# A hybrid encoder trunk in one program: the convolution's layer norm in two stages, w_out's split spread over attention units, and three more taps off VectorE

## The chip, the cores and the metric

The kernel runs on one core of one Trainium2 chip, as one launch. The metric is the device time of the launch in microseconds, as the median of several executions. A profile of one execution gives the trace from which all durations come; its span runs from the first instruction to the last. In the profile PE is TensorE's matmuls, PEld its weight loads, DVE is VectorE, ACT is ScalarE, POOL is GpSimd and SP issues the DMAs.

## The reference, cut to what matters

One layer of an encoder, run for a prompt of 512 rows and a sample of 1024 rows with the same weights, model width 1024:

```python
h = rmsnorm(x, norm_attn_g)
z = h @ w_in                                   # q, k, v, ca, cb
a_out = window_attn(q, k, v, bias, band, sink) # 8 heads of 64, blocks of 128, each sees 3 blocks
c = ca * sigmoid(cb)
c = dwconv(c, conv_dw_w, conv_dw_b)            # 31 taps along the rows, 512 channels
c = silu(layernorm(c, conv_ln_g, conv_ln_b))   # over the 512 channels of a row
x = x + concat(a_out, c) @ w_out
h = rmsnorm(x, norm_ffn_g)
u = dwconv(h @ w_up, ffn_dw_w, ffn_dw_b)       # 3 taps, 2 x 2816 channels
x = x + (silu(u[:, :2816]) * u[:, 2816:]) @ w_down
y = rmsnorm(x, norm_final_g)
```

All of it is float32. The kernel makes each float32 product from three matmuls of rounded parts: a high part, and a low part that is the rest (`hi*hi + hi*lo + lo*hi`). So every operand of a product is split first: a cast on ACT gives the high part, a subtraction on POOL or DVE the low part.

## The kernel before, in words

The work is cut in blocks of 128 rows: blocks 0 to 3 are the prompt, 4 to 11 the sample. An attention unit u is one block (u // 2) and one of two key heads (u % 2), so units 0 to 7 are the prompt's and 8 to 23 the sample's.

**Stages.** First come the input projections of the prompt, then those of the sample with the prompt's attention, convolution norm and output projection between them. Then follows the prompt's FFN up-projection, 22 steps (`ffn_step`), with the sample's attention between its matmuls. Behind it come the sample's output projections (`out_half`), the convolution norms of its later blocks, and the FFN of the sample, whose order is written out by hand and which the change does not touch.

**Side work.** Work beside the main stream is written as generators that yield between pieces. `proj`, the loop over 24 matmuls of a projection, calls `tick()` three times, and its caller once more. A tick adds `rate` to a due count and advances the first generator of `side` for each whole one; and it adds a credit, of which each convolution item takes its cost of 0.66. `convs` holds the items of the prompt, `late` those of the sample, which are served when `convs` is empty. The program order that comes out is laid onto the engines' queues by a planner that works ahead of time with its own timeline; on the chip each engine's queue is in order.

**Convolution.** `conv_items(g, c, cp)` makes one column block of 128 channels and 512 rows: 31 taps less `NOFF[g]` are `scalar_tensor_tensor` on DVE into a PSUM bank (L339), the last `NOFF[g]` are a scaling on ACT (L328, L331) and an add on POOL (L332). The result goes to DRAM (`cvd`).

**Convolution norm.** `conv_norm(i)` loads one block of `cvd` (L669), transposes it (L675), takes statistics on DVE (L677, L678) and the inverse root on POOL (L173, L174), scales on DVE (L681), yields twice (`YN`), transposes back (L687), applies gain, bias and silu on ACT and DVE (L690 to L693) and splits (L694, L695) into `cats[i, 1]`. For the prompt it first drains `convs`. It is called whole: behind units 4 to 7 for blocks 0 to 3, for blocks 4 and 5 behind the sample's attention (`NE` = 2), and for block i + 2 beside the output projection of block i.

**Attention and w_out.** `attention(u0, u1, then)` runs `scores(u + 1)`, `values(u)`, then the generator `then[u]`. `w_out` has 16 tiles of 128 x 512; each is loaded (L736, L738) and split (`split_wo`, L740, on ACT and POOL through L189 and L190). For the sample, `sample()` does this in one loop after all attention units, five loads ahead of the splits (`WOA`). `w_up` is split by the same L189 and L190, one half of a column block after each half of an FFN step.

**Memory.** SBUF tiles come from counted slots; h is the class of 61 slots of 2 KB. PSUM is eight banks, of which projections take two, attention and norm three to five.

Of the kernel before, what the change touches and what calls it, by code (L numbers as in the profile page):

```python
# [36 lines left out]

RA, RB, RBO, RD, RN, RE = 1.2, 0.8, 2.5, 0.8, 0.95, 0.9  # L40


CA, CB = 0.9, 0.4
CL, CLO, CD = 0.6, 1.0, 0.6

NOFF = (4, 7)

SCB, SCD = "aapa", "aaap"


WOP, WOA, DW, DW2 = 1, 5, 2, 0
NE = 2
YN = 2
OB = "uc"
VG = 3
NW = 36
KEEP = 3
U0 = 2

# [83 lines left out]
def tile_hybrid_encoder(ctx: ExitStack, tc: tile.TileContext, xs, rel_bias, norm_attn_g, w_in,  # L143
# [9 lines left out]

    sb = Slots(big, dict(q=(15, 4096), c=(4, 4224), h=(61, 2048), d=(2, 2176), s=(32, 64)), "q", KEEP)
    banks = Slots(lambda tag: ps[two_of[tag]], dict(a=(3, 2048), u=(2, 2048), b=(2, 2048), c=(1, 2048)))
    use = dict(step="aub", turn="aub", conv="c", attn="au", norm="b", out="b", up="u", down="b")
# [4 lines left out]
    def bank(job):  # L161
        return banks.tile([NT], among=use[job])
# [51 lines left out]
    def rows_T(parts, out):  # L214
        r = sb.tile([P])
        n = 0
        for src, k in parts:
            nc.sync.dma_start(r[n:n + k, :], src)
            n += k
        pt = bank("step")  # L220
        nc.tensor.transpose(pt[:, :n], r[:n, :], ident[:n, :n])
        nc.vector.tensor_copy(out, pt[:, :n])
# [3 lines left out]
    rows_T([(rw(norm_attn_g), 8)], vecs[:, 0:8])  # L226
    for _ in range(NW // 4):
        pt = bank("step")
        for i in range(4):
            nc.tensor.transpose(pt[:, i * P:(i + 1) * P], ident[:], ident[:])  # L230
        pt = None
# [33 lines left out]
    side, pace = deque(), dict(rate=0.0, due=0.0, conv=0.0, credit=0.0, late=0.0)  # L265

    def advance(queue):
        try:
            return next(queue[0])
        except StopIteration:  # L270
            queue.popleft()
            return 0.0
# [15 lines left out]
    def drain(queue):  # L288
        while queue:
            advance(queue)  # L290
# [24 lines left out]
    def conv_items(g, c, cp):  # L315
        T = GR[g]["T"]
        w = lambda t: cvw[:, t * 4 + c:t * 4 + c + 1]
        cost = 0.13 + NT / 960.0
        noff = NOFF[g]
        off = list(range(CK - noff, CK))  # L320
        for n in range(T // NT):
            src = lambda t: cp[:, t + n * NT:t + (n + 1) * NT]
            pacc = sb.tile([NT])

            def offload(k):
                t = off[k]
                if k == 0:
                    nc.scalar.activation(pacc[:], src(t), AF.Identity, scale=w(t))  # L328
                else:
                    pr = sb.tile([NT])  # L330
                    nc.scalar.activation(pr[:], src(t), AF.Identity, scale=w(t))  # L331
                    nc.gpsimd.tensor_tensor(pacc[:], pacc[:], pr[:], op=ALU.add)  # L332

            acc = bank("conv")
            nc.vector.tensor_scalar(acc[:], src(0), w(0), cvb[:, c:c + 1], op0=ALU.mult, op1=ALU.add)
            yield cost
            k = 0
            for t in range(1, CK - noff):
                nc.vector.scalar_tensor_tensor(acc[:], src(t), w(t), acc[:], op0=ALU.mult, op1=ALU.add)  # L339
                if t % 2 == 1 and k < noff:  # L340
                    offload(k)
                    k += 1
                yield cost
            while k < noff:
                offload(k)
                k += 1
            nc.vector.tensor_tensor(pacc[:], acc[:], pacc[:], op=ALU.add)
            del acc
            nc.sync.dma_start(cvd[g][:, c, n * NT:(n + 1) * NT], pacc[:])
            yield cost  # L350

    tanh_t, cpads, kt, vt = {}, {}, {}, {}
# [150 lines left out]
    bias = []  # L503
# [12 lines left out]
    NB = len(blocks)  # L516
    qt, cats, units = {}, {}, {}
# [13 lines left out]
    score_rows = []  # L531

    def sink_columns():
        for h in range(0, NH, 2):
            t = sb.tile([2, NT])
            for n in range(2):
                nc.vector.tensor_copy(t[:, n, 0:1], nsink[:, h + n:h + n + 1])
            score_rows.append(t)
# [60 lines left out]
    def cat_of(i, part):  # L599
        if (i, part) not in cats:  # L600
            cats[i, part] = (sb.tile([4, P], F32R), sb.tile([4, P], F32R))
        return cats[i, part]
# [46 lines left out]
    def attention(u0, u1, then={}):  # L649
        yield from scores(u0)  # L650
        for u in range(u0, u1):
            if u + 1 < u1:
                yield from scores(u + 1)
            yield from values(u)
            if u in then:
                yield from then[u]

    def load_cat(i):
        cats[i, 0] = (sb.tile([4, P], F32R), sb.tile([4, P], F32R))
        for L in range(2):  # L660
            nc.sync.dma_start(cats[i, 0][L][:].bitcast(F32), catd[blocks[i][1], :, L, :].rearrange("p (j t) -> p j t", t=P))

    def conv_norm(i):
        G, b = blocks[i]
        if G["g"] == 0:
            drain(convs)
        cat = cat_of(i, 1)
        cv = sb.tile([4, P])
        nc.sync.dma_start(cv[:], cvd[G["g"]][:, :, b * P:(b + 1) * P])  # L669
        if G["g"] == 1 and (i, 0) not in cats:  # L670
            load_cat(i)
        yield 0.0
        pt = bank("norm")
        for c in range(4):
            nc.tensor.transpose(pt[:, c * P:(c + 1) * P], cv[:, c, :], ident[:])  # L675
        st, mv, rs = sm(6), sm(2), sm(1)
        nc.vector.bn_stats(st[:], pt[:])  # L677
        nc.vector.bn_aggr(mv[:], st[:])  # L678
        rstd_of(mv[:, 1:2], 1.0, rs[:])
        xh = sb.tile([CCH])  # L680
        nc.vector.tensor_scalar(xh[:], pt[:], mv[:, 0:1], rs[:], op0=ALU.subtract, op1=ALU.mult)  # L681
        del pt
        for _ in range(YN):
            yield 0.0
        p2 = bank("norm")
        for c in range(4):
            nc.tensor.transpose(p2[:, c * P:(c + 1) * P], xh[:, c * P:(c + 1) * P], ident[:])  # L687
        y, t = sb.tile([4, P]), sb.tile([4, P])
        for c in range(4):
            nc.scalar.activation(y[:, c, :], p2[:, c * P:(c + 1) * P], AF.Identity,  # L690
                                 scale=lng[:, c:c + 1], bias=lnb[:, c:c + 1])
        nc.scalar.activation(t[:], y[:], AF.Tanh)
        nc.vector.scalar_tensor_tensor(t[:], t[:], 1.0, y[:], op0=ALU.add, op1=ALU.mult)  # L693
        nc.scalar.copy(cat[0][:], t[:])  # L694
        nc.vector.tensor_tensor(cat[1][:], t[:], cat[0][:].bitcast(F32), op=ALU.subtract)  # L695
        yield 0.0
# [70 lines left out]

    use.update(step="b", turn="a", attn="au", norm="au", out="u")

    def prompt():  # L770
        yield from attention(0, 8, {u: conv_norm(u - 4) for u in range(4, 8)})
        kt.clear(), vt.clear(), qt.clear(), bias.clear()
        pace.update(rate=RBO, late=CLO)
        for n in range(2):
            for kc in range(KC):
                if (kc, n) not in wor:
                    load_wo(kc, n)
            yield 0.0
            for kc in range(KC):
                split_wo(kc, n, kc % 2 < DW)  # L780
                if kc % 2 == 1:
                    yield 0.0
            for i in range(4):
                if n == 0 and i == 3:
                    for kc in range(WOP):
                        load_wo(kc, 1)
                yield from out_half(i, n)
            wo.clear()
        yield from make_h2(0, 0)
# [107 lines left out]
        want_up(0, half)  # L897
    want_up_raw(1, 0)
    load_bias()
    def sample():  # L900
        sink_columns()
        yield from attention(8, 24)
        kt.clear(), vt.clear(), qt.clear(), bias.clear(), score_rows.clear()
        use.update(norm="a")
        pace.update(rate=RN)
        for m in range(16 + WOA):
            if m in (10, 12):
                load_cat(m // 2 - 1)
            if m < 16:
                load_wo(m // 2, m % 2)  # L910
            if m >= WOA:
                split_wo((m - WOA) // 2, m % 2, m % 4 < DW2)
                yield 0.0
        drain(late)
        for m in range(NE):
            yield from conv_norm(4 + m)

    pace.update(rate=RD, late=CD)
    for k in range(NJ):
# [159 lines left out]
    pace.update(rate=2.2)  # L1079
    for i in range(4, NB - 2):  # L1080
        if i + NE < NB:
            side.appendleft(conv_norm(i + NE))
        if i == 8:
            pace.update(rate=RE)
            side.appendleft(turned(1, old_bank))
        for n in range(2):
            out_blocks(i, n)
# [155 lines left out]
    for j in range(2):  # L1243
        st[j] = dict(x=wide())
        prod(st[j]["x"][:, L], j, 1, True, True)
        a = sb.tile([NT])
# [322 lines left out]
    u, e, o11, o12 = (acc.pop(n) for n in ("u", "e", "o11", "o12"))  # L1569
# [73 lines left out]
```

## Time and profile before

| | us |
|---|---|
| median of 3 runs (lowest, highest) | 1564.2 (1560.03, 1566.33) |
| the profiled execution's own time | 1558.91 |
| its span | 1557.1 |
| TensorE busy | 1506.9 (97%) |
| VectorE busy | 1126.2 (72%) |
| ScalarE busy | 795.4 (51%) |
| GpSimd busy | 708.9 (46%) |

The granted clock of TensorE is 0.990 of full speed over the span. A row of a group has a line, an engine, an operation, output and inputs by name, and a count; then durations, or the idle time before them and what ended it. Where windows are shown, each gives its length, then for each engine the busy time and in brackets the instructions, then the granted clock, the share of the DMA engines' time and GB/s.

### The profile page before, as it was taken

How to read it: one execution, taken by the hardware profiler on the slowest of the kernel's cores; microseconds unless marked ns; L12 is line 12 of the kernel's file. 1: busy time of each engine (PE TensorE's matmuls, PEld its weight loads, DVE VectorE, ACT ScalarE, POOL GpSimd, SP SyncE). 2: the span in 40 equal slices, each digit the busy share in tenths (PEclk: the TensorE clock that was granted, in tenths of full speed). 3: DMA queues.
4: the chain of work that ended last, by engine and by line, in shares of the span. 5: the costliest groups of instructions: out<-in, count | busy, mean ns of one | idle time of the engine just before them, and what ended most of it. 6: DMA issues, size and time to landing. Idle time of an engine off the chain costs nothing. (4 is left out here: it accounts for less than half of the span.)

```text
span 1557.1 us, 20112 instructions
## 1 busy us (share of the span) xinstructions
PE 1506.9 (97%) x6843; PEld 1229.4 (79%) x6843; DVE 1126.2 (72%) x1604; ACT 795.4 (51%) x1404; POOL 708.9 (46%) x566
## 2 busy tenths in 40 slices
PE   8899998999999999899999999999999999999997
PEld 6787787787888888777777888888888788888885
DVE  7999767857788785344868777777776845568883
ACT  4634654335787786633454444455545543444254
POOL 7652344226666776947433455555554000003355
PEclk9999999999999999999999999999999999999999
DMA  7582334447343346779332233333331582356644
GB/s 230 156 212 81 107 100 124 129 142 217 112 132 129 118 129 181 242 238 298 114 93 76 92 104 104 105 104 102 102 115 64 200 284 82 105 165 230 221 135 162
DMA packets 228780, 227.17 MB, mean 146 GB/s; under 512 B 13268, under 2 KB 168348, under 8 KB 228549
## 3 DMA queue, kind: packets, MB, share of 16 engines
q1 hardware_dynamic: 228677, 225.88, 45.8%
q8 instruction: 54, 0.88, 0.2%
q14 instruction: 49, 0.40, 0.1%
HBM read 164.74 MB, written 62.14 MB: 146 GB/s over the span
## 5 line engine op out<-in xcount | busy, mean ns | idle before, releaser
L190 POOL TENSOR_TENSOR q<-q,q 128x1024 fp32r<-128x1024 f32 x72 | 173.4, 2415 | 93.4 <-ACT q L189 34.4
L940 POOL TENSOR_TENSOR q<-q,q 128x512 fp32r<-128x512 f32 x101 | 140.0, 1391 | 164.0 <-ACT q L1050 151.7
L940 DVE TENSOR_TENSOR h<-h,h 128x512 fp32r<-128x512 f32 (+2 forms) x202 | 153.9, 794 | 65.2 <-ACT h L944 25.3
L1398 PE MATMUL w<-h,h 128*128 128x512 f32 x462 | 181.4, 393 | 1.4 <-DVE q L1185 1.4
L1399 PE MATMUL w<-h,h 128*128 128x512 f32 x462 | 181.5, 393 | 0.0
L1400 PE MATMUL w<-h,h 128*128 128x512 f32 x462 | 181.1, 392 | 0.0
L1064 PE MATMUL w<-h,q 128*128 128x512 f32 x448 | 176.5, 394 | 1.0 <-ACT h L1147 0.6
L1066 PE MATMUL w<-h,q 128*128 128x512 f32 x448 | 175.5, 392 | 1.0 <-POOL q L940 1.0
L1065 PE MATMUL w<-h,q 128*128 128x512 f32 x426 | 166.4, 391 | 0.0
L296 PE MATMUL u<-h,q 128*128 128x512 f32 x400 | 161.0, 403 | 5.4 <-DVE h L837 4.1
L297 PE MATMUL u<-h,q 128*128 128x512 f32 x400 | 158.6, 397 | 0.0
L299 PE MATMUL u<-h,q 128*128 128x512 f32 x384 | 151.8, 395 | 2.7 <-POOL q L190 2.7
L937 POOL TENSOR_TENSOR q<-q,q 128x1024 f32<-128x1024 f32 x12 | 32.4, 2707 | 236.6 <-DVE q L937 220.0
L339 DVE SCALAR_TENSOR_TENSOR c<-c,cvw,c 128x512 f32<-128x512 f32 x184 | 138.0, 750 | 2.9
L944 ACT CAST h<-h 128x512 fp32r<-128x512 f32 x120 | 71.9, 619 | 93.2 <-DVE h L940 41.9
L296 PE MATMUL b<-h,q 128*128 128x512 f32 x256 | 102.7, 401 | 3.3 <-DVE d L369 2.2
L1398 PEld LDWEIGHTS w<-h,h 128*128 128x128 f32 x462 | 86.8, 188 | 21.6 <-ACT h L944 1.8
L1400 PEld LDWEIGHTS w<-h,h 128*128 128x128 f32 x462 | 86.7, 188 | 19.7
L1399 PEld LDWEIGHTS w<-h,h 128*128 128x128 f32 x462 | 86.8, 188 | 19.5
L837 DVE SCALAR_TENSOR_TENSOR h<-u,fw,h 128x511 f32<-128x511 f32 x88 | 65.5, 744 | 49.8 <-ACT h L841 49.0
L299 PE MATMUL b<-h,q 128*128 128x512 f32 x256 | 101.4, 396 | 0.0
L297 PE MATMUL b<-h,q 128*128 128x512 f32 x256 | 101.1, 395 | 0.0
(417 smaller groups left out, 3670.4 us busy)
## 6 DMA issues: line engine op xcount, KB each, us to landing
q<-in_w_up SPq DMA_DIRECT2D x88, 512.0 KB
ga<-q SPq DMA_DIRECT2D x64, 256.0 KB
h<-ga SPq DMA_DIRECT2D x57, 256.0 KB
q<-in_w_in SPq DMA_DIRECT2D x28, 512.0 KB
h<-in_w_down SPq DMA_DIRECT2D x52, 256.0 KB
q<-in_x_sample SPq DMA_DIRECT2D x15, 512.0 KB
h<-qsd SPq DMA_DIRECT2D x24, 256.0 KB
x1d<-q SPq DMA_DIRECT2D x11, 512.0 KB
```

The source lines that it names most:

```text
L190: (nc.vector if dve else nc.gpsimd).tensor_tensor(lo[:], raw[:], hi[:].bitcast(F32), op=ALU.subtract)
L296: nc.tensor.matmul(out, whi[:, kc, :], hi[:], start=(kc == 0), stop=False)
L297: nc.tensor.matmul(out, whi[:, kc, :], lo[:], start=False, stop=False)
L299: nc.tensor.matmul(out, wlo[:, kc, :], hi[:], start=False, stop=(kc == KC - 1))
L339: nc.vector.scalar_tensor_tensor(acc[:], src(t), w(t), acc[:], op0=ALU.mult, op1=ALU.add)
L940: (eng or nc.vector).tensor_tensor(out, a, b, op=ALU.subtract)
L1064: nc.tensor.matmul(out, whi[:, s], hi[:], start=(start and c == 0), stop=False, **go)
L1065: nc.tensor.matmul(out, whi[:, s], lo[:], start=False, stop=False, **go)
L1066: nc.tensor.matmul(out, wlo[:, s], hi[:], start=False, stop=(stop and c == 3), **go)
L1398: nc.tensor.matmul(out, sh[:, c], th[:], start=(p == 0), stop=False)
L1399: nc.tensor.matmul(out, sh[:, c], tl[:], start=False, stop=False)
L1400: nc.tensor.matmul(out, sl[:, c], th[:], start=False, stop=(p == NPAIR - 1))
```

## The change

`conv_norm` is cut in two. `conv_norm_1` runs up to the scaled rows, which it keeps in `normed`; `conv_norm_2` transposes them back and does the rest. For the prompt, the first stage of block i stands behind unit i + 3, the second behind unit i + 4, ahead of the next block's first. For the sample, the first stages of blocks 4 and 5 follow the splits, then second and first stages alternate, two blocks apart; beside the output projection of block i stand the second stage of i + 2 and the first of i + 4.

The loop over w_out's tiles becomes a generator, of which two pieces are taken behind each of units 19 to 23 and the rest after the attention.

`NOFF` goes from 4 to 7 for the prompt's four column blocks, and from 7 to 10 for the first two of the sample's (both halves of the rows). Convolution credits for the sample go from 0.6, 1.0 and 0.6 a tick to 0.45, 0.8 and 0.62; the side rates `RD` and `RN` from 0.8 and 0.95 to 0.84 and 0.9.

```diff
-RA, RB, RBO, RD, RN, RE = 1.2, 0.8, 2.5, 0.8, 0.95, 0.9
+RA, RB, RBO, RD, RN, RE = 1.2, 0.8, 2.5, 0.84, 0.9, 0.9
-CL, CLO, CD = 0.6, 1.0, 0.6
-NOFF = (4, 7)
+CL, CLO, CD = 0.45, 0.8, 0.62
+NOFF = ((7, 7, 7, 7), (10, 10, 7, 7))
-YN = 2
+WOU = 19
-        noff = NOFF[g]
+        noff = NOFF[g][c]
+    normed = {}
     def conv_norm(i):
+        yield from conv_norm_1(i)
+        yield from conv_norm_2(i)
+    def conv_norm_1(i):
...
         nc.vector.tensor_scalar(xh[:], pt[:], mv[:, 0:1], rs[:], op0=ALU.subtract, op1=ALU.mult)
-        del pt
-        for _ in range(YN):
-            yield 0.0
+        normed[i] = xh
+        yield 0.0
+    def conv_norm_2(i):
+        cat, xh = cat_of(i, 1), normed.pop(i)
         p2 = bank("norm")
...
     def prompt():
-        yield from attention(0, 8, {u: conv_norm(u - 4) for u in range(4, 8)})
+        yield from attention(0, 8, {u: both(*([conv_norm_2(u - 4)] if u > 3 else []), *([conv_norm_1(u - 3)] if u < 7 else []))
+                                    for u in range(3, 8)})
...
-    def sample():
-        sink_columns()
-        yield from attention(8, 24)
-        kt.clear(), vt.clear(), qt.clear(), bias.clear(), score_rows.clear()
-        use.update(norm="a")
-        pace.update(rate=RN)
+    def wo_pieces():
         for m in range(16 + WOA):
...
+    def some(gen, n):
+        for _ in range(n):
+            if next(gen, None) is None:
+                return
+            yield 0.0
+    def sample():
+        sink_columns()
+        wos = wo_pieces()
+        yield from attention(8, 24, {u: some(wos, 2) for u in range(WOU, 24)})
+        kt.clear(), vt.clear(), qt.clear(), bias.clear(), score_rows.clear()
+        use.update(norm="a")
+        pace.update(rate=RN)
+        yield from wos
         drain(late)
+        yield from conv_norm_1(4)
+        yield from conv_norm_1(5)
         for m in range(NE):
-            yield from conv_norm(4 + m)
+            yield from conv_norm_2(4 + m)
+            if NE + 4 + m < NB:
+                yield from conv_norm_1(4 + NE + m)
...
         if i + NE < NB:
-            side.appendleft(conv_norm(i + NE))
+            side.appendleft(both(conv_norm_2(i + NE), *([conv_norm_1(i + NE + 2)] if i + NE + 2 < NB else [])))
```

More of the change, by code (lines that the diff above doesn't have):

```diff
@@ L666, in conv_norm @@
             drain(convs)
-        cat = cat_of(i, 1)
         cv = sb.tile([4, P])
@@ L768, in tile_hybrid_encoder, with both @@
     use.update(step="b", turn="a", attn="au", norm="au", out="u")
+    def both(*gens):
+        for g in gens:
+            yield from g
     def prompt():
-        yield from attention(0, 8, {u: conv_norm(u - 4) for u in range(4, 8)})
+        yield from attention(0, 8, {u: both(*([conv_norm_2(u - 4)] if u > 3 else []), *([conv_norm_1(u - 3)] if u < 7 else []))
+                                    for u in range(3, 8)})
         kt.clear(), vt.clear(), qt.clear(), bias.clear()
```

## The prediction

> **What bounds the kernel now.** I read the page's busy times first, then the list of what TensorE waited for, then the windows around the waits, and last the timeline inside the two worst windows.
>
> ```profile
> PE 1506.9 (97%) x6843; PEld 1229.4 (79%) x6843; DVE 1126.2 (72%) x1604; ACT 795.4 (51%) x1404; POOL 708.9 (46%) x566
> ```
>
> TensorE is busy 1506.9 of 1557.1 us, so nothing that leaves its 6843 instructions alone can win more than the 50.2 us in which it stands, plus what it loses at a lowered clock. The change adds and removes no TensorE instruction. It can only fill holes or make new ones, and only up to the last convolution norm's activation:
>
> ```profile
> L690 ACT ACTIVATE h<-a,vecs x36: 441/457/488, 240.8 to 764.6; 128x128 f32<-128x128 f32 x36
> ```
>
> That is at 764.6 us. The list of TensorE's waits names the holes (wait, total, times, longest):
>
> ```profile
> PE u L296 <- DVE h L837: 4.1, 2, 3.5
> PE u L687 <- DVE q L681: 4.0, 1, 4.0
> PE u L687 <- DVE h L681: 2.9, 1, 2.9
> PE u L711 <- DVE s L678: 2.2, 1, 2.2
> PE b L296 <- DVE d L369: 2.2, 1, 2.2
> PE u L616 <- DVE s L567: 2.0, 2, 1.1
> PE a L560 <- DVE s L567: 1.7, 1, 1.7
> PE a L675 <- DMA h<-cvd: 1.4, 1, 1.4
> PE b L987 <- DVE q L958: 1.0, 1, 1.0
> ```
>
> L687 are the second transposes of the convolution norm, which wait for the normalised rows of L681. L711 is the output projection, which comes right behind a norm. L296 behind L837 is an up-projection waiting for its PSUM bank. The windows show what each place costs in all (length, then busy times of PE, PEld, DVE, ACT, POOL, the granted clock, DMA):
>
> ```profile
> 267.00:281.00 14.00, 7.03 (x27) 5.35 (x25) 6.60 (x12) 8.32 (x17) 7.67 (x9) 0.63 0.39 118
> 281.00:290.00 9.00, 9.00 (x40) 7.27 (x40) 6.48 (x11) 4.95 (x9) 0.75 (x2) 1.00 0.75 228
> 560.00:629.00 69.00, 69.00 (x341) 57.81 (x341) 46.06 (x94) 52.67 (x102) 49.34 (x30) 1.00 0.56 169
> 629.00:665.00 36.00, 31.91 (x136) 25.36 (x135) 11.89 (x18) 20.00 (x32) 35.84 (x26) 0.95 0.71 225
> 680.00:690.00 10.00, 7.81 (x34) 6.22 (x33) 6.00 (x9) 4.70 (x9) 6.06 (x9) 0.83 1.05 370
> 730.00:740.00 10.00, 8.55 (x43) 6.76 (x42) 4.43 (x6) 1.77 (x3) 5.09 (x7) 1.00 0.97 311
> 740.00:750.00 10.00, 8.32 (x41) 6.41 (x40) 6.33 (x9) 5.03 (x11) 5.66 (x9) 1.00 0.65 217
> ```
>
> **The prompt's norms (L663 to L695).** The timeline of 267 to 280 us, block 2's norm (start, duration, engine, line):
>
> ```profile
> 267.06 0.60 PE L675 MATMUL a<-ident,q 128*128 128x128 f32 x4
> 268.60 1.26 POOL L332 TENSOR_TENSOR q<-q,q 128x512 f32<-128x512 f32 x1 [3.29 <-ACT q L331]
> 270.22 0.57 POOL L174 TENSOR_TENSOR s<-s,nhalf 128x1 f32<-128x1 f32 x1
> 270.83 0.81 DVE L681 TENSOR_SCALAR q<-a,s,s 128x512 f32<-128x512 f32 x1 [2.21 <-POOL s L174]
> 271.69 1.12 PE L687 MATMUL u<-ident,q 128*128 128x128 f32 x4 [4.03 <-DVE q L681]
> 272.85 1.50 ACT L690 ACTIVATE h<-u,vecs 128x128 f32<-128x128 f32 x4 [2.23 <-PE u L687]
> 276.61 1.09 PE L687 MATMUL u<-ident,h 128*128 128x128 f32 x4 [2.94 <-DVE h L681]
> 279.70 0.60 ACT L373 ACTIVATE h<-b 128x512 fp32r<-128x512 f32 x1
> ```
>
> The two transposes stand next to each other on TensorE with a whole chain between them: statistics, the root on POOL behind a convolution add (L332), the scaling on DVE. Projections cannot fill the gap, because their bank is emptied by L373, which sits in ACT's queue behind L690, which waits for L687. That is a knot of in-order queues, and it is tied twice, for blocks 2 and 3.
>
> What does it cost? The 14.00 us hold 27 TensorE instructions. Sixteen are transposes, 0.60 us for four at full clock (row at 267.06). Eleven are matmuls, at 9.00/40 = 0.225 us each when nothing is missing (281 to 290). That is 2.4 + 2.5 = 4.9 us of work, so 9.1 us are lost, 6.97 of them standing and the rest at the clock of 0.63.
>
> The change puts an attention unit between the stages: L687 of block i comes directly behind values(i+4), with its rows ready since values(i+3). The second stage of one block then meets only the first stage of the next. Nothing is added but a held tile per block. Both waits on L681 should go. What stays is the ACT work ahead of L373 (L690 and three more for each block), so I leave 2.6 us of the 9.1 and book **-6.5** (bounds -9.1, where all goes, and 0, where the knot is tied at another place). Next in the queue is then the output projection, 5 ticks earlier in program order, because the two stages together yield 12 times where the old norm yielded 16 times.
>
> **w_out's splits (L740, cast L189 and subtract L190).** Sixteen splits come in one run behind the attention, and POOL is busy 35.84 of 36.00 us there. ACT suffers with it:
>
> ```profile
> 651.70 0.62 ACT L189 CAST h<-h 128x512 fp32r<-128x512 f32 x1 [1.32 <-DMA h<-in_w_out]
> 653.26 0.77 ACT L841 ACTIVATE h<-u,vecs,fw 128x512 f32<-128x512 f32 x1
> 655.75 0.76 PE L296 MATMUL u<-h,q 128*128 128x512 f32 x1 [3.45 <-DVE h L837]
> ```
>
> ACT stands 1.32 us for a w_out tile that has not landed, behind it wait L841 and L837, and TensorE waits for the bank they free. The window loses 4.09 us standing and 0.05 x 36 = 1.8 at the lowered clock, 5.9 in all. The change moves ten of the sixteen splits to units 19 to 23, with loads two or three units ahead: 5.9 x 10/16 = **-3.7** (bounds -5.9 and 0). The cover of the moved work is POOL's and ACT's idle time at 560 to 629 us: a split is one L190 on POOL, so ten are 13.0 us by the row below, against 69.00 - 49.34 = 19.7 us idle; 16.3 us of ACT are idle there, too. If that cover fails, see the second rival.
>
> **The norms of the sample.**
>
> ```profile
> 684.95 0.47 PE L711 MATMUL u<-h,h 128*128 128x512 f32 x1 [2.19 <-DVE s L678]
> 685.25 0.40 PE L712 MATMUL u<-h,h 128*128 128x512 f32 x1
> 687.84 0.63 PE L711 MATMUL u<-h,h 128*128 128x512 f32 x1
> ```
>
> In 680 to 690 us stand 12 transposes (1.8 us) and 22 matmuls (4.95), so 3.2 us are lost: 2.19 standing and 1.0 to the slow matmuls behind it (0.63 against 0.40). The norms of blocks 4 and 5 will be finished and those of 6 and 7 begun when the first output projection starts, and w_out is done 30 matmuls earlier. I book **-2.5** (bounds -3.2 and 0). In 730 to 750 us 3.1 us stand open, but the list's two waits there, L675 for the convolution's rows (1.4) and L987 for a DVE scaling (1.0), stay where they are: **-0.5** (bounds -3.1 and +1).
>
> The clock behind a hole is where trace and skill part. The Trainium skill (TensorE: Matmul & The Clock Gate, "HAM oscillation — how this bites in real kernels") says that gaps longer than about 3.4 us bring the slow clock; by that the 2.19 us gap would cost only itself, this term would be -1.5, and the sum 1.0 us less. Here the row at 687.84 shows slow matmuls behind it, so the measurement decides.
>
> **Taps.** Twelve taps of the prompt and twelve of the sample leave DVE and become a scaling on ACT and an add on POOL:
>
> ```profile
> L339 DVE SCALAR_TENSOR_TENSOR c<-c,cvw,c x184: 714/752/758, 184.2 to 575.8; 128x512 f32<-128x512 f32 x184
> L331 ACT ACTIVATE h<-c,cvw x38: 707/722/737, 230.4 to 581.2; 128x512 f32<-128x512 f32 x38
> L332 POOL TENSOR_TENSOR h<-h,h x47: 1278/1297/2162, 41.5 to 585.5; 128x512 f32<-128x512 f32 x47
> L190 POOL TENSOR_TENSOR h<-h,h x16: 1282/1302/1314, 629.2 to 664.9; 128x512 fp32r<-128x512 f32 x16
> ```
>
> Per twelve: DVE -9.0 us (0.752 each), ACT +8.7 (0.722), POOL +15.6 (1.297). For the sample they fall, by the order of ticks, beside the prompt's output projections and before the sample's attention; in 281 to 290 us POOL is busy 0.75 of 9.00 us there, ACT 4.95: 0. For the prompt they fall ahead of 190 us. There TensorE waits 5.9 us for DVE (2.2 + 2.0 + 1.7 in the list), which could shrink, but POOL's weight splits stand in the queue with the added adds: six adds of the first two channel blocks are 7.8 us. The convolution's credit per tick is as before, so DVE is as dense as before and only done sooner (forced out 8 ticks earlier, with 10 taps left, not 17). I take **0** (bounds -5.9 and +7.8; nearer the first row, as the taps run in a spare queue most of the time).
>
> ```profile
> 50.39 0.75 DVE L247 TENSOR_SCALAR q<-q,s 128x1024 f32<-128x1024 f32 x1 [0.44 <-POOL s L174]
> 60.48 2.40 DVE L247 TENSOR_SCALAR q<-q,s 128x1024 f32<-128x1024 f32 x1
> ```
>
> The same scaling took 0.75 and, beside a POOL split, 2.40 us, which speaks against more work on POOL; but the taps of L339 stay within 714 to 758 ns whatever POOL does, so only the few L247 can be hit. The Trainium skill (SBUF — State Buffer, "SBUF: two separate sides") has DVE and POOL lock a shared port for a whole instruction; were every DVE instruction hit, the 15.6 us would outweigh the 9.0 by 6.6 and the sum would be 6.6 us smaller. The rows of L339 say otherwise.
>
> **The rest.** New rates and credits add no instruction: 0. Any of these edits reorders the queues up to 765 us, and tiles are held longer (ten early pieces take some 25 of the 61 small tiles, of which 17 to 28 are free in units 19 to 23, so SP's w_out loads may wait for a slot with w_up loads behind them). I allow for two new waits like those of L616, 1.0 each: **+2.0** (bounds 0 and +6).
>
> **Sum.** -6.5 - 3.7 - 2.5 - 0.5 + 0 + 2.0 = -11.2 us. The profiled execution took 1558.9 us, 1.8 around its span of 1557.1; it would take 1547.7. The median of the runs shown is 1564.2, 5.3 above the profiled one, so I put the same difference on the median: **1553.0 us**.
>
> **Rivals.** *The knot stays.* The second stage meets another in-order wait, or the first stage's L675 takes the wait, and the prompt gains nothing: -4.7, 1559.5 us. For it: the queues' order is worked out ahead of time, and in front of L687 stands whatever its plan thinks ready. Against: L681 would be finished a whole unit before L687.
>
> *POOL becomes the bound in units 19 to 23: slower.* Two splits per unit put 2.60 us in POOL's queue, and if they stand ahead of a w_up split, TensorE waits for it.
>
> ```profile
> 603.34 2.41 POOL L190 TENSOR_TENSOR q<-q,q 128x1024 fp32r<-128x1024 f32 x1 [5.37 <-issue]
> 610.41 0.39 PE L296 MATMUL u<-h,q 128*128 128x512 f32 x1
> ```
>
> A w_up split that ends at 605.75 is used at 610.41: 4.66 us of lead. It decides from the point where the splits and whatever queues behind them eat that lead. Then each of five units costs 2.6 us standing and 1.0 of slow clock behind it, 18.0 in all, and the sample's gains fail too as POOL is late again at 629: 18.0 - 6.5 = +11.5, 1575.7 us. Against: POOL's 19.7 idle us there, and the lead.
>
> *Every hole closes:* 9.1 + 5.9 + 3.2 + 3.1 + 5.9 = 27.2 off, 1537.0 us.
>
> **How the numbers follow.** A measurement of this kernel can tell about 0.5%, 7.8 us, from no change. The forecast has 0.55 (0.02 of it above 1556.4), the knot 0.20, POOL 0.20, all holes 0.05. Faster: 0.55 - 0.02 + 0.05 = 0.58; same: 0.22; slower: 0.20. The forecast's own range is 1544 to 1562 (prompt gain 0 to 9.1, taps -5.9 to +4). To leave out no more than 2 in 10, I go from 1540, which drops most of the last case, to 1574, which drops half of POOL's: 0.15 left out.
>
> **What would show it.** Right: no wait of L687 for L681 in the prompt, the clock at 1.00 from 267 to 281 us, POOL clearly under 36 of 36 us around 629 to 665, no wait of L296 for L837 and none of L711 behind a norm, with DVE's busy time down by 18 and POOL's up by 31 us. Wrong: TensorE waiting for L190 at 560 to 629 us, new waits in front of L675, or a sum of TensorE's standing time ahead of 765 us no smaller than now.

## The result, and the profile after

The changed kernel takes **1577.3 us** (median, 1573.1 to 1578.7) against 1562.9 us of the kernel before (four runs of each): a ratio of **1.0086 [1.0061, 1.0111]**, slower. The profiled execution took 1576.8 us; its span is 1574.9, 17.8 longer than before.

The busy line of the page and the list of what TensorE waited for, of the kernel after:

```profile
PE 1518.0 (96%) x6843; PEld 1237.1 (79%) x6843; DVE 1115.5 (71%) x1580; ACT 811.4 (52%) x1428; POOL 739.6 (47%) x590
```

```profile
PE u L296 <- DVE h L851: 8.7, 3, 7.1
PE u L560 <- DMA h<-qsd: 3.9, 1, 3.9
PE u L560 <- DVE q L640: 3.9, 1, 3.9
PE u L720 <- ACT h L189: 3.3, 1, 3.3
```

Of the 17.8 us, TensorE's busy time holds 11.1 (1518.0 against 1506.9 for the same 6843 instructions, at a mean granted clock of 0.982 against 0.990), and standing 6.7 (56.9 against 50.2). The wait of the second transposes for the scaled rows (now L696 and L687) is gone, and so is that of the output projection (now L720) for a statistic. Of the four waits shown, that of L296 for its bank has grown from 4.1 us and that of L560 for q from 0.4; the other two are new. How late the stream is at two marks can be read from one group, the activations of the FFN steps (count, durations in ns, first and last start); it is L841 before and L855 after:

```profile
L841 ACT ACTIVATE h<-u,vecs,fw x44: 755/778/797, 376.4 to 686.3; 128x512 f32<-128x512 f32 x44
```

```profile
L855 ACT ACTIVATE h<-u,vecs,fw x43: 758/779/790, 389.4 to 708.1; 128x512 f32<-128x512 f32 x43
```

So 13.0 us are lost ahead of the FFN, 8.8 more by its end (21.8 there), and 4.0 come back behind it (17.8 at the span's end). The windows name the places, first before, then after. They are cut by the clock, and as the stream runs late after, a window does not hold quite the same work in both:

```profile
120.00:130.00 10.00, 7.93 (x41) 6.69 (x42) 8.18 (x25) 5.35 (x18) 0.93 (x1) 1.00 0.39 119
240.00:260.00 20.00, 19.26 (x94) 15.53 (x93) 17.63 (x33) 13.93 (x30) 8.26 (x5) 1.00 0.67 176
260.00:290.00 30.00, 23.03 (x97) 18.36 (x96) 16.34 (x26) 14.32 (x27) 10.81 (x11) 0.83 0.52 156
290.00:300.00 10.00, 10.00 (x45) 8.22 (x44) 9.73 (x13) 2.36 (x4) 3.37 (x2) 1.00 0.43 129
665.00:690.00 25.00, 22.81 (x101) 18.49 (x100) 10.07 (x16) 6.08 (x11) 9.29 (x13) 0.93 0.73 245
```

```profile
120.00:130.00 10.00, 6.08 (x25) 4.88 (x24) 8.53 (x19) 2.45 (x8) 0.00 (x0) 0.82 0.79 239
240.00:260.00 20.00, 15.11 (x65) 12.20 (x64) 15.10 (x32) 10.65 (x23) 4.57 (x5) 0.83 0.49 119
260.00:290.00 30.00, 28.17 (x133) 22.80 (x131) 20.57 (x31) 18.65 (x34) 17.38 (x12) 1.00 0.68 181
290.00:300.00 10.00, 8.54 (x26) 6.79 (x27) 2.81 (x3) 4.78 (x8) 4.58 (x4) 0.66 0.23 63
629.00:665.00 36.00, 35.63 (x169) 29.00 (x168) 14.78 (x29) 20.91 (x38) 27.47 (x18) 1.00 0.56 183
665.00:690.00 25.00, 17.88 (x71) 13.91 (x71) 8.50 (x12) 10.66 (x15) 18.43 (x13) 0.86 0.46 146
730.00:750.00 20.00, 20.00 (x90) 16.30 (x89) 8.53 (x11) 7.29 (x15) 15.29 (x20) 1.00 1.03 356
```

The change did what it was to do where it was to do it: 260 to 290 us went from 97 to 133 TensorE instructions, 629 to 665 us from 31.91 to 35.63 us busy with POOL at 27.47 instead of 35.84, and 730 to 750 us hold no gap, where 3.1 us stood open. But there are new holes: 120 to 130 us (16 instructions fewer), and next to the first two gains 240 to 260 (29 fewer), 290 to 300 (19 fewer) and 665 to 690 (30 fewer).

The hole at 243 us, in the timeline after, engine by engine, shows how the knot was tied again:

```profile
240.15 0.62 ACT L189 CAST h<-h 128x512 fp32r<-128x512 f32 x1 [2.86 <-DMA h<-in_w_out]
240.68 0.63 ACT L701 ACTIVATE d<-h 128x512 f32<-128x512 f32 x1
242.13 0.72 ACT L331 ACTIVATE h<-c,cvw 128x512 f32<-128x512 f32 x1 [0.82 <-DVE d L702]
...
243.00 1.27 POOL L332 TENSOR_TENSOR h<-h,h 128x512 f32<-128x512 f32 x1 [9.22 <-ACT h L331]
...
245.64 0.69 DVE L347 TENSOR_TENSOR h<-c,h 128x512 f32<-128x512 f32 x1 [2.55 <-POOL h L332]
...
246.86 0.69 DVE L640 TENSOR_TENSOR q<-u,h 64x512 f32<-64x512 f32 x1
...
247.70 0.77 PE L560 MATMUL u<-h,h 128*128 128x256 f32 x2 [3.89 <-DVE q L640]
```

Read from the end: TensorE waits 3.89 us for attention's L640; L640 stands on DVE behind L347, the sum of a column block; L347 waits for the last taps' adds on POOL; these for a scaling L331 on ACT. The scaling waits last for L702 on DVE, the step behind the tanh of a norm's second stage (L701), and the tanh stands in ACT's queue behind the cast of a w_out tile (L189), for which ACT stood 2.86 us. So three things meet in one queue: a second stage and a moved tap, which are edits, and a cast of w_out, which follows from the first, as the output projections stand earlier in program order (from 220 to 262 us ACT has one cast of w_out before, at 223.14, and three after).

### The profile page after: what moved, and what is told of

It is laid out like the page before. It is cut to its first block, busy times and chain, and to the rows that moved or that the text cites. A ratio compares the mean times of both kernels' runs of the same rounds, so it can differ in the third digit from the quotient of the medians.

```text
span 1574.9 us, 20211 instructions
## 1 busy us (share of the span) xinstructions
PE 1518.0 (96%) x6843; PEld 1237.1 (79%) x6843; DVE 1115.5 (71%) x1580; ACT 811.4 (52%) x1428; POOL 739.6 (47%) x590
## 5 line engine op out<-in xcount | busy, mean ns | idle before, releaser
L190 POOL TENSOR_TENSOR q<-q,q 128x1024 fp32r<-128x1024 f32 x71 | 170.3, 2403 | 98.9 <-ACT q L189 32.4
L296 PE MATMUL u<-h,q 128*128 128x512 f32 x400 | 162.8, 407 | 10.0 <-DVE h L851 8.7
L299 PE MATMUL u<-h,q 128*128 128x512 f32 x376 | 150.1, 399 | 0.8 <-POOL q L190 0.8
L339 DVE SCALAR_TENSOR_TENSOR c<-c,cvw,c 128x512 f32<-128x512 f32 x172 | 128.9, 749 | 2.1
L332 POOL TENSOR_TENSOR h<-h,h 128x512 f32<-128x512 f32 x64 | 85.1, 1332 | 65.6 <-ACT h L331 60.2
L189 ACT CAST q<-q 128x1024 fp32r<-128x1024 f32 x72 | 75.4, 1049 | 64.3 <-POOL q L190 13.0
L296 PE MATMUL b<-h,q 128*128 128x512 f32 x256 | 104.0, 406 | 2.1 <-DVE d L369 1.8
L1426 PEld LDWEIGHTS w<-h,h 128*128 128x128 f32 x462 | 86.8, 188 | 20.9 <-issue 0.9
L1092 PEld LDWEIGHTS w<-h,q 128*128 128x128 f32 x448 | 84.6, 189 | 23.6 <-ACT h L1175 2.2
L299 PE MATMUL b<-h,q 128*128 128x512 f32 x256 | 102.7, 401 | 0.0
L1427 PEld LDWEIGHTS w<-h,h 128*128 128x128 f32 x462 | 86.8, 188 | 19.9
```

Source lines behind the costliest of these rows:

```text
L190: (nc.vector if dve else nc.gpsimd).tensor_tensor(lo[:], raw[:], hi[:].bitcast(F32), op=ALU.subtract)
L296: nc.tensor.matmul(out, whi[:, kc, :], hi[:], start=(kc == 0), stop=False)
L299: nc.tensor.matmul(out, wlo[:, kc, :], hi[:], start=False, stop=(kc == KC - 1))
L1092: nc.tensor.matmul(out, whi[:, s], hi[:], start=(start and c == 0), stop=False, **go)
L1426: nc.tensor.matmul(out, sh[:, c], th[:], start=(p == 0), stop=False)
L1427: nc.tensor.matmul(out, sh[:, c], tl[:], start=False, stop=False)
```

## Experiments

Each is the kernel before with parts of the change, or the changed kernel with parts taken out. Ratios are against the kernel before; 0.001 is 1.6 us.

**Each part alone.** The first four say which part costs. e1, the prompt's taps:

```diff
-NOFF = (4, 7)
+NOFF = ((7, 7, 7, 7), (7, 7, 7, 7))
```

> The kernel before with only the prompt's taps changed (4 to 7 of 31 to ACT and POOL). Theory T (taps): the changed kernel is 12.5 us behind when the FFN starts because six more adds and scalings stand in POOL's and ACT's queues ahead of the weight splits and q evacuations; then this kernel alone is slower by 5 to 10 us, all of it before 260 us. Rival N (norm): the taps are free and the two-stage norm with its earlier output projections makes the 12.5; then this is within 2 us. Rival R (reordering): the planner's order is what moves; then the sign is open and the loss sits at waits that have nothing to do with L332.

Measured: 1572.5 us, 1.0062 [1.0041, 1.0083]. Slower by about 9.7 us. In the traces 8.6 us are there when the FFN starts (385.0 against 376.4 us for the first row of the group above); this trace is of the longest of e1's four executions and ends 16.5 us behind. More on the taps is below (e12). e2, the prompt's two-stage norms, with `conv_norm` cut as in the change:

```diff
+        yield from attention(0, 8, {u: both(*([conv_norm_2(u - 4)] if u > 3 else []), *([conv_norm_1(u - 3)] if u < 7 else []))
+                                    for u in range(3, 8)})
```

> The kernel before with only the prompt's norm in two stages, a unit apart; the sample's norm, w_out, taps and rates as before. The prediction's term: 6.5 us faster, no wait of L687 for L681. Theory N: 3 to 8 us slower, as the first output projection now waits for w_out (3.3 us in the changed kernel). Theory T: 4 to 8 us faster, since only the taps cost.

Measured: 1586.9 us, 1.0152 [1.0134, 1.0171]. This part alone costs more than the whole change, and three times what theory N allowed. The longest wait, with the ACT rows ahead of it:

```profile
303.53 1.04 ACT L189 CAST q<-q 128x1024 fp32r<-128x1024 f32 x1 [3.77 <-DMA q<-in_w_in]
304.48 0.61 ACT L189 CAST h<-h 128x512 fp32r<-128x512 f32 x1
...
305.14 1.22 PE L755 MATMUL u<-h,h 128*128 128x512 f32 x2 [9.92 <-ACT h L189]
```

The output projection (L755 here) comes up before its w_out tile is cast, and that cast stands behind a split of w_in that waits for its load. e3, the spread:

```diff
...
+        wos = wo_pieces()
+        yield from attention(8, 24, {u: some(wos, 2) for u in range(WOU, 24)})
```

> The kernel before with only w_out's splits spread over units 19 to 23. Theory P (POOL and the w_up slots): slower by 6 to 10 us, lost between 560 and 680 us, with up-projections waiting for L837 and ACT's cast waiting for w_up to land. Prediction's term: 3.7 us faster. Rival: the loss of 9 us in the changed kernel comes from the rates and the earlier norms there; then within 2 us.

Measured: 1564.3 us, 1.0004 [0.9989, 1.0018]. The spread alone neither gains nor loses. e4, the sample's two-stage norms:

```diff
+        yield from conv_norm_1(4)
+        yield from conv_norm_1(5)
         for m in range(NE):
-            yield from conv_norm(4 + m)
+            yield from conv_norm_2(4 + m)
+            if NE + 4 + m < NB:
+                yield from conv_norm_1(4 + NE + m)
...
+            side.appendleft(both(conv_norm_2(i + NE), *([conv_norm_1(i + NE + 2)] if i + NE + 2 < NB else [])))
```

> The kernel before with only the sample's norms in two stages. The changed kernel gains 7 us between 690 and 760 us; if that is the two stages alone, this is 4 to 7 us faster, with no wait of the output projection for L678 and none of L687. If it came from w_out being split earlier, within 2 us.

Measured: 1559.3 us, 0.9970 [0.9956, 0.9983]. The sample's two-stage norms gain 4.7 us alone.

**The prompt's two-stage norms taken apart.** They do three things at once: the norm is cut, the convolution is forced out behind unit 3 instead of 4, and the output projections start five ticks earlier. Four kernels vary these, each on the kernel before. The first, e5, adds only a delay to e2:

```diff
+        for _ in range(4):
+            yield 0.0
```

> The kernel before with the prompt's two-stage norms alone, plus four empty yields behind the prompt's attention, so that the output projections start at the tick at which they start in the kernel before. The two-stage norms alone took 22.5 us more than the kernel before; their longest wait (9.9 us) is the output projection's for a split of w_out. Theory O (the projections come before w_out is split): that wait goes and with it most of the loss, 0 to +8 us against the kernel before. Theory D (the convolution is forced out a unit earlier and crowds VectorE): only the wait goes, +10 to +16 us. Theory S (the split of the norm itself is bad for the queues): as D, +10 to +16 us.

Measured: 1574.5 us, 1.0070 [1.0043, 1.0096]. The wait of 9.9 us is gone, and with it 12.8 us (1.0152 to 1.0070): rather more than half of the loss is the earlier output projection. The rest stays, so theory O is not enough. e6 puts both stages a unit later (block 3 has both behind unit 7) and keeps the delay:

```diff
+        yield from attention(0, 8, {u: both(*([conv_norm_2(u - 5)] if u > 4 else []), conv_norm_1(u - 4), *([conv_norm_2(3)] if u == 7 else []))
+                                    for u in range(4, 8)})
+        for _ in range(4):
+            yield 0.0
```

> The kernel before with the prompt's norms in two stages, but each stage a unit later: the first stage of block i behind unit i + 4, where the whole norm stood, the second behind unit i + 5 (block 3: both behind unit 7), and the same four empty yields. So the convolution is forced out at the old tick, and the output projections start at the old tick. Theory D: nothing of the loss is left, and some of the 6.5 us booked for the knot may be won: -7 to +2 us against the kernel before. Theory O: the same, -7 to +2. Theory S: still +10 or more.

Measured: 1560.8 us, 0.9978 [0.9961, 0.9995]. Cutting the norm does no harm in itself: kept a unit later, with projections at their old tick, it gains 3.4 us on this kernel. Theory S falls. e7 only forces the convolution out early:

```diff
+    def early():
+        drain(convs)
+        yield from ()
...
+        yield from attention(0, 8, {3: early(), **{u: conv_norm(u - 4) for u in range(4, 8)}})
```

> The kernel before with one call more: the prompt's convolution is forced out behind unit 3 instead of in the first norm, behind unit 4. The norms are whole, and nothing else moves. Theory D: +10 to +18 us against the kernel before, with VectorE dense with taps from 210 to 300 us. Theories O and S: -3 to +3 us.

Measured: 1565.3 us, 1.0007 [0.9989, 1.0024]. Theory D, as it was put, falls as well: forcing the convolution out early costs nothing when the norms are whole. e11 joins the calls of e6 and e7:

> The prompt's two-stage norms a unit later (alone -4 us), with the one call added that forces the convolution out behind unit 3 (alone 0). If the 10 us that the change's positions still lost with the projections at their old tick come from forcing the convolution out early together with two stages: +8 to +12 us against the kernel before. If they come from the place of the first stages themselves, a unit earlier among the prompt's last attention units: -5 to +2.

Measured: 1570.5 us, 1.0038 [1.0020, 1.0057], 9.4 us more than e6. So it is the two together: an early end of the convolution costs 0.7 thousandths beside whole norms and 6.0 beside cut ones. The rest up to e5 (3.2 thousandths, with intervals that overlap) may be the place of the first stages, a unit earlier; that is not shown. The window of 220 to 260 us, in the order before, e6, e7, e11 and e5:

```profile
220.00:260.00 40.00, 39.09 (x188) 31.50 (x187) 31.48 (x59) 25.68 (x54) 17.92 (x13) 1.00 0.58 150
```

```profile
220.00:260.00 40.00, 40.00 (x199) 33.24 (x198) 28.94 (x53) 25.93 (x54) 15.37 (x14) 1.00 0.71 189
```

```profile
220.00:260.00 40.00, 36.12 (x178) 29.30 (x176) 38.24 (x70) 25.31 (x58) 13.00 (x11) 1.00 0.55 146
```

```profile
220.00:260.00 40.00, 35.17 (x160) 28.26 (x159) 35.06 (x64) 22.84 (x49) 10.70 (x10) 0.92 0.62 166
```

```profile
220.00:260.00 40.00, 34.14 (x146) 26.86 (x145) 36.62 (x64) 24.24 (x53) 13.90 (x12) 0.83 0.48 129
```

In e6 DVE is busy 28.94 us and TensorE never stands. In e11 and e5 DVE is busy 35 to 37 of 40 us, and TensorE executes 39 and 53 instructions fewer. Of the same window L339's rows alone (the taps on DVE), in e6 and e11:

```profile
220.00:260.00 40.00, 8.42 (x12) 1.00 0.71 189
```

```profile
220.00:260.00 40.00, 18.87 (x26) 0.92 0.62 166
```

In e6 12 taps fall here, in e11 26. But many taps alone do not cost the time: before has 20 of them here and e7 27. In e7 DVE is busy 38.24 us and TensorE stands 3.9, little less than the 4.8 of e11, but the clock stays full, and over its runs e7 is not slower. What e11 and e5 have besides are the cut norms. The likely reading is that attention and the stages of the norm pass through DVE in short steps, each now behind a tap, while TensorE's queue holds few projections between them (19 of their matmuls at 240 to 260 us in e5, 75 in e6, 66 in e7); no run shows that alone.

**The change with parts taken out.** e8 has the prompt's norms whole:

> The changed kernel with the prompt's norms whole again, all else as changed (taps, w_out's spread, the sample's two-stage norms, rates and credits). If the parts add up as they measured alone (taps +8, spread 0, sample's norms -5): about +3 us against the kernel before, 1567 us, which is 11 us less than the changed kernel. If the prompt's two-stage norm cost its 22.5 us inside the change, too: 1555 us. Rival (the taps' delay ahead of 200 us and the new credits carry the loss of the change): no less than 1573 us.

Measured: 1570.7 us, 1.0040 [1.0022, 1.0058], between the forecasts of 1567 and 1573 us. The FFN starts at 377.2 us instead of 389.4. Inside the change the prompt's norms thus cost 4.6 thousandths, 7.2 us. What is left in its trace was lost behind 560 us: the FFN's activations run 0.6 us behind those of before at 560 us and 12.5 at the last. e10 takes the spread out of e8:

```diff
-WOU = 19
+WOU = 24
```

> The changed kernel with the prompt's norms whole again (1570.7 us) and, in addition, no spread of w_out's splits: the loop starts behind the last attention unit, as before. What is left of the change are the taps, the sample's two-stage norms, and rates and credits. If the spread costs the 10 us that TensorE falls behind between 580 and 690 us in the run with the spread, of which 690 to 770 us give half back: about 1565 us. If it costs nothing there, as alone (0): 1570 us.

Measured: 1562.2 us, 0.9987 [0.9967, 1.0006]. The spread, free alone, costs 5.3 thousandths, 8.3 us, in company, more than either forecast had. Its hole in the changed kernel (e8 has the same, with 7.06 us), by SP, ACT and TensorE:

```profile
665.28 0.38 SPq L183 DMA_DIRECT2D q<-in_w_up  x1
...
668.93 1.06 ACT L189 CAST q<-q 128x1024 fp32r<-128x1024 f32 x1 [4.44 <-DMA q<-in_w_up]
...
679.52 0.76 PE L296 MATMUL u<-h,q 128*128 128x512 f32 x1 [7.12 <-DVE h L851]
```

A load of w_up is issued at 665.28 us, ACT stands 4.44 us for it, and behind it in ACT's queue come the activations L855 of the FFN step, so the bank comes free late. The load itself stood 5.1 us on SP, until TensorE's last product with an earlier tile (L299) was done, so it was not behind a load of w_out. Is it GpSimd's queue, or the late load? e13 puts the subtractions of e8's splits on DVE:

```diff
-WOP, WOA, DW, DW2 = 1, 5, 2, 0
+WOP, WOA, DW, DW2 = 1, 5, 2, 4
```

> The changed kernel with the prompt's norms whole again (1.0040 of the kernel before; without the spread 0.9987) and the subtractions of w_out's sixteen splits on VectorE instead of GpSimd, which takes some 21 us from GpSimd between 590 and 680 us. If the spread costs because its splits stand in GpSimd's queue with those of w_up: the ratio comes back to 0.998 to 1.000, and the up-projection's wait of 7.1 us near 670 us goes. If it costs because of tiles held and loads that come late on the queue of DMAs: the ratio stays at 1.003 to 1.006 with that wait.

Measured: 1566.3 us, 1.0012 [0.9999, 1.0025]: about half of the 5.3 thousandths came back, between the two forecasts (the intervals of e8 and e13 just overlap). The windows of 629 to 690 us, with the spread (e8), without (e10), and with the spread on DVE (e13), and e13's longest wait:

```profile
629.00:690.00 61.00, 51.37 (x226) 40.56 (x225) 23.16 (x38) 29.35 (x52) 40.50 (x29) 0.92 0.47 153
```

```profile
629.00:690.00 61.00, 54.56 (x238) 43.40 (x237) 22.84 (x35) 26.01 (x42) 40.28 (x31) 0.97 0.65 187
```

```profile
629.00:690.00 61.00, 50.72 (x220) 40.64 (x220) 35.99 (x47) 28.56 (x52) 26.82 (x17) 0.92 0.48 154
```

```profile
662.32 0.79 PE L296 MATMUL u<-h,q 128*128 128x512 f32 x1 [5.93 <-ACT q L189]
```

GpSimd went from 40.50 to 26.82 us, and this window is no better: TensorE waits 5.93 us for a cast of w_up, and ACT stood 3.15 of them for its load. So w_up's load still comes late when GpSimd is relieved. Whether the spread makes it late, and what gave back the other half, is not settled by these lines.

**The taps.** e12 moves only those of two column blocks:

```diff
-NOFF = (4, 7)
+NOFF = ((4, 4, 7, 7), (7, 7, 7, 7))
```

> The kernel before with seven taps off VectorE, not four, for the last two column blocks of the prompt only (all four: +8 us). If the loss comes from the scalings that stand in ScalarE's queue ahead of the first unit's q, at 105 to 127 us: 0 to +2 us, as those belong to the first two blocks. If every tap moved costs alike (GpSimd and ScalarE busy): +4 us.

Measured: 1563.6 us, 0.9994 [0.9982, 1.0007]. The taps of the last two column blocks are free alone, so the loss of e1 needs those of the first two. Its trace shows a place where the stream falls behind (ACT, DVE and TensorE; first e1, then before):

```profile
110.24 0.72 ACT L331 ACTIVATE h<-q,cvw 128x512 f32<-128x512 f32 x1 [3.41 <-DMA qsd<-h]
...
112.21 0.60 ACT L373 ACTIVATE h<-a 128x512 fp32r<-128x512 f32 x1 [0.76 <-PE a L299]
...
116.71 0.68 DVE L374 SCALAR_TENSOR_TENSOR h<-a,h 128x512 fp32r<-128x512 f32 x1
...
127.56 0.76 PE L560 MATMUL u<-h,h 128*128 128x256 f32 x2 [4.23 <-DMA h<-qsd]
```

```profile
105.13 0.72 ACT L331 ACTIVATE h<-q,cvw 128x512 f32<-128x512 f32 x1 [4.34 <-DMA qsd<-h]
...
110.63 0.59 ACT L373 ACTIVATE h<-a 128x512 fp32r<-128x512 f32 x1
...
112.41 0.68 DVE L374 SCALAR_TENSOR_TENSOR h<-a,h 128x512 fp32r<-128x512 f32 x1
...
120.42 0.48 PE L560 MATMUL u<-h,h 128*128 128x256 f32 x2 [0.44 <-DMA h<-qsd]
```

The first scores come 7.1 us later and TensorE stands 4.23 us for q to come back; in e12 they come at 117.4 us. A scaling waits 3.41 us on ACT for a small tile that still holds q on its way out, but before has such a wait, too, of 4.34 us, so the wait alone is not the loss. The high part of q's last column block (L373) is 1.6 us later than before, its low part (L374), behind six taps on DVE, 4.3, and SP issues the two loads of q (L524) 3.6 and 6.8 us later (115.55 and 123.27 against 112.00 and 116.51). Which of these steps costs what, no run separates. In company most of the delay is made up later: e8 has the same taps, its first scores come at 126.5 us, and its FFN still starts at 377.2.

**Putting it together.** e9 has both pairs of norms, the prompt's as in e6:

> The kernel before with two-stage norms in both places and nothing else: the prompt's a unit later than in the change, with the output projections at their old tick (alone -4 us), and the sample's as in the change (alone -5 us). If the two gains are in different places and add up: -9 us, 1555 us, and faster than both kernels. Rival (each only shifts the same holes to another place): -5 us or less.

Measured: 1561.9 us, 0.9989 [0.9977, 1.0000]. Both pairs of norms, -3.4 and -4.7 alone, give -1.7 together. Gains of this size don't add up here; that each edit sets the order of all that follows anew is the likely reason. e14 is e8 with two edits:

```diff
-NOFF = ((7, 7, 7, 7), (10, 10, 7, 7))
+NOFF = ((4, 4, 7, 7), (10, 10, 7, 7))
-WOU = 19
+WOU = 24
```

> The changed kernel without the three parts that cost time: the prompt's norms whole, no spread, and the extra taps of the prompt on the last two column blocks only. It keeps the sample's two-stage norms, the sample's taps, rates and credits. If the costs were found rightly: 0.992 to 0.998 of the kernel before (0.9987 with the taps, less part of the 8 us that the first two blocks' taps cost alone). If those taps cost nothing in this company: 0.9987.

Measured: 1555.5 us, **0.9947 [0.9934, 0.9961]**, faster than both kernels. Against e10 that is 4.0 thousandths, 6.3 us, for the taps of the prompt's first two blocks. e15 is the same with the prompt's norms as in e6:

> As the run before, but the prompt's norms stay in two stages, a unit later than in the change, and the output projections start at their old tick. If the two-stage norms of the prompt gain here as alone (-4 us): 0.990 to 0.996 of the kernel before. If they gain nothing beside the sample's, as when only the two pairs of norms were joined (0.9989): the same as the run before, or slower by up to 4 us.

Measured: 1556.9 us, 0.9956 [0.9942, 0.9970]: beside the rest, cutting the prompt's norms no longer gains.

## Why the prediction was wrong

**The sum.** Taken out of the changed kernel one after the other, the prompt's norms are worth +7.2 us (e8), w_out's spread +8.3 (e10) and the first two blocks' taps +6.3 (e14); what remains is worth -8.3. Together that is, but for rounding, the +13.4 of the change. The prediction had -6.5, -3.7, 0 and, for the rest (the sample's norms and the allowance), -1.0. So three terms came out as costs. Each was priced by the wait or the engine that it was to relieve, and not by what moved with the step.

**The prompt's norms, -6.5: the step that failed most.** The mechanism was right as far as it went: the second transposes no longer wait for the scaled rows, and the norm cut without its company gains 3.4 us (e6). What failed is the upper bound of 0, "where the knot is tied at another place". The prediction itself named the two things that came with the cut, the output projection five ticks earlier and the convolution forced out eight ticks earlier, and charged nothing for either. The first costs 12.8 us (e2 against e5), the second 9.4 beside cut norms (e11 against e6). Alone the step is +23.8 us, inside the change +7.2. Why it costs less there was not run; DVE has only 7 taps at 220 to 260 us in the changed kernel, and its wait comes through the moved ones instead, as the chain at 243 us shows. The first rival (the second stage meets another in-order wait) had the mechanism, but priced it as a gain lost, not as a cost.

**w_out's splits, -3.7: the second step that failed.** Right where it looked: 629 to 665 us is nearly full and POOL is at 27.47. Wrong in the sum: 0 alone (e3), +8.3 in company (e8 against e10). The wait of L296 for the bank did not go; it moved behind 665 us and grew from 3.5 to 7.1. The prediction had late loads of w_up in mind, but behind loads of w_out, and only in an allowance of 2.0; the load at 665.28 us was held by TensorE's use of a tile, and why the spread costs in company stays half open. The rival on POOL had the right sign and the wrong place: TensorE never waits for L190 at 560 to 629 us, and with the splits on DVE a long wait stays (e13). That its 1575.7 us lies next to the measured 1577.3 is chance.

**The sample's norms, -3.0.** Right: -4.7 [-6.9, -2.7] alone, and no gap from 730 to 750 us in the changed kernel.

**Taps, 0 (bounds -5.9 and +7.8).** The taps' own time on DVE fell as reckoned, by 18.1 us in 24 instructions, and POOL's rose by 30.7 us, but the prompt's taps alone made the time 9.7 us longer [6.4, 13.0], which reaches the upper bound of 7.8 and more, and in company those of two blocks 6.3. The bound looked at GpSimd's queue; the rows show q late instead, by steps on ACT, DVE and SP that no run separates (e1, e12).

**The parts alone.** 9.7 + 23.8 + 0.6 - 4.7 makes +29 us; the change is +13.4. The rates, the credits and the sample's taps, booked at 0, were not run alone; with the sample's norms and the taps of the prompt's last two blocks they make the -8.3 us of e14.

**What was to show it.** The wait on L681, POOL at 629 to 665 and L711 came out as forecast; the clock at 260 to 290 did, too. The wait of L296 for the bank stayed, and TensorE's standing time did not get smaller (40.5 us ahead of 765 us, 35.4 before), which the prediction had named as the sign of its failure.

One caution for reading all this: the trace of the kernel before is of an execution 4 us under its median (1558.9 us), so a single trace can't tell effects of that size. e6 starts its FFN 1.2 us later than that trace, and is still 0.9978 over the runs. The trace of e3, whose edit lies behind that point, starts its FFN 4.5 us later. Verdicts on small effects here rest on the ratios, and the traces only say where.

## What to carry to other kernels

When a step is moved in a program whose order comes from ticks and in-order queues, price what moves with it: the work it forces out, and the stage behind it that now starts before its operands are ready. A wait between two neighbours can be cut and cost more than it gives, unless what follows and what is forced out stay where they were: here the same cut was +23.8 us or -3.4. Work taken off a busy engine goes into another's queue; look at what stands behind it there, not at that engine's share. And measure a part by leaving it out as well as alone, as the two differ: the spread was +0.6 us alone and +8.3 in company.

## What the hardware showed

Small DVE operations can be held for as long as a GpSimd operation runs. The two additions of the softmax's denominator, of 128 x 4 elements, before and after (count, then shortest, median and longest in ns):

```profile
L583 DVE TENSOR_TENSOR s<-sinkb,s x8: 141/158/163, 124.4 to 246.4; 128x4 f32<-128x4 f32 x8
L588 DVE TENSOR_TENSOR s<-s,s x8: 154/159/754, 126.9 to 250.7; 128x4 f32<-128x4 f32 x8
```

```profile
L583 DVE TENSOR_TENSOR s<-sinkb,s x8: 151/156/2162, 130.4 to 259.0; 128x4 f32<-128x4 f32 x8
L588 DVE TENSOR_TENSOR s<-s,s x8: 150/158/1865, 131.9 to 259.7; 128x4 f32<-128x4 f32 x8
```

And in e5, DVE beside POOL:

```profile
237.41 1.08 DVE L583 TENSOR_TENSOR s<-sinkb,s 128x4 f32<-128x4 f32 x1
...
239.07 2.29 DVE L588 TENSOR_TENSOR s<-s,s 128x4 f32<-128x4 f32 x1
```

```profile
236.06 2.41 POOL L190 TENSOR_TENSOR q<-q,q 128x1024 fp32r<-128x1024 f32 x1
...
238.94 2.39 POOL L190 TENSOR_TENSOR q<-q,q 128x1024 fp32r<-128x1024 f32 x1
```

Each addition ends within 0.03 us of a split on POOL (238.49 and 238.47, 241.36 and 241.33). The prediction thought that only the few L247 could be hit. The Trainium skill (SBUF — State Buffer, "SBUF: two separate sides") has the shared port as an exclusive lock for a whole instruction, which a DVE operation with two SBUF inputs meets when GpSimd reads SBUF; these rows agree, and so do the taps of L339, which accumulate in PSUM and keep their 714 to 760 ns. The sixteen additions took 3.4 us in all before and 8.6 after, which is part of why DVE's busy time fell by 10.7 us and not by 18.

The clock fell without a long gap. In e5 TensorE stood 0.89, 1.68, 0.67 and 1.11 us between 243 and 254 us, never longer, and the granted clock of that stretch is 0.65:

```profile
243.00:255.00 12.00, 7.17 (x25) 5.11 (x23) 11.29 (x21) 8.97 (x21) 2.74 (x4) 0.65 0.36 89
```

So short gaps one after the other are enough: here 4.83 us of standing come with about 2.5 us of slower matmuls (an estimate, 0.35 of 7.17). The Trainium skill (TensorE: Matmul & The Clock Gate, "HAM oscillation — how this bites in real kernels") speaks of gaps above about 3.4 us; here the measurement decides.
